# A sample's recurrent steps cut in two, and mixed with the last chunk of a head

## The chip, the cores and the metric

The kernel runs on one core of a Trainium2 chip. The metric is the device time of one execution in microseconds. Its engines are named as in the profile: PE is TensorE's matmuls and PEld its weight loads, DVE is VectorE, ACT is ScalarE, POOL is GpSimd, and SP is SyncE, which issues most of the transfers.

## The reference

The kernel computes one step of a two-layer decoder for a prompt of 2048 positions and eight samples of four tokens each (32 rows). Layer A, in which the change lies, is a gated linear attention with four heads, keys of 128 and values of 512. Per head the prompt runs from a zero state; each sample starts from a stored state of its own.

```python
log_a = log_sigmoid(g_low @ w_gate2 + b_gate) / 16
# per chunk of positions, per head
b   = cumsum(log_a)
rel = where(causal, b[t] - b[s], -inf)
scores[t, s] = sum_d q[t, d] * k[s, d] * exp(rel[t, s, d])
out   = (q * exp(b)) @ state + scores @ v
state = exp(b_last) * state + (k * exp(b_last - b)).T @ v
# per head: RMS norm of out, then
y = (norm(out) * silu(gate)) @ w_out
```

Layer B (windowed attention on shared keys and values) follows; the change does not touch it. Outputs are both groups' activations, the new states and the new caches.

## The kernel before, in words

Products are done in f16 with each f32 operand split in a high and a low part (`split`, lines 194 and 195, or 197 and 198 with a scale: ACT writes the high part, then DVE the low one), in three passes of matmuls. All matmuls are issued through line 101.

Layer A walks over 16 blocks: four heads, and for each the four blocks of 512 positions of the prompt, in the loop over `blocks`. A block projects `q` and `k` (`pj`, copied out at line 430 as `qT`, `kT`), `v` and the gate (`v` is a `split`; the gate's `sg` is a tanh at line 477 and a product at 478), computes the decay's running sum in `logs` (Abs, Exp and Ln on ACT at lines 366 to 368, a sum, a product and a scan on DVE at 370 to 372), the scores by levels, and then four chunks of 128 positions. A block's products are woven (`weave(main, fill)`: the fill's steps spread evenly among the main's) with the next block's levels and with the chunk before.

The last block of a head also makes `SampleA(h)`: the head's projections for the 32 sample rows (`proj_steps`), and a list of steps for their recurrence:

- `diag`: the sample's decay logs (`logs` with 32 columns, tile `E` 128x32, scan into `sbt`), the split of q and k, and the diagonal of the scores `S`;
- `level(0, 2)` and `level(1, 1)`: exponents of decay differences (`k1`, shown as `k`), an Exp on ACT (line 723), products with q and k, the split into `ssm` (194 and 195), three matmuls into `lev`, and a copy into `S`;
- `mid`: the scores' split `Sh`, q with its decay, Exp at line 741, and the factors `ebs`;
- `stack`: keys and values stacked for three passes, transposed, and the first matmul into the readout `o`;
- eight times `seq(b)`: load of the sample's state (`W`, two samples in one transfer; in the last head `bt`, one each), its split into `pst`, three matmuls of it into `o`, one for the update into `kv`, the decay of the state on ACT (line 795), the sum on DVE, and the store;
- `fin`: norm and gate, into `ogTs`.

The first four steps are put behind the last chunk's steps of the head (`prev_tail`) and woven with the `v` and `sg` projections of the next head's first block; the other ten are spread over that block's three remaining chunks. In the last head all of them go into the steps of the output projection.

Two things set the order of the work around the change. Each engine runs its queue in order, so that an instruction which waits holds all behind it on that engine. And the queues themselves come from a scheduler that takes the program's order as priority: an instruction stands where its inputs and buffers are expected, the earlier step first; some steps (the conversion of later weights, through `pst` and `pre`) are put 200 places back in priority. Buffers are few: two PSUM buffers `pj`, one each of `lev` and `kv`, two of `tr` and `o`, two `E`, two `pst`, twelve `W`, three `wraw`, one `S`, one `ssm`, one `sq2`, two `bt`.

Weights come in through `wraw` (issued on SP at line 223), are scaled and split into `W` (197 and 198), and free `wraw` for the next load. A state load of the sample stands behind such loads on SP.

Of the kernel before, what the change touches and what calls it, by code (L numbers as in the profile page):

```python
# [74 lines left out]
def _body(tc, nc, cp, sb, ps, dr, i, o):  # L75
# [6 lines left out]
    def T(tag, shape, dt, bufs=None):  # L82
        return sb.tile(shape, dt, tag=tag, name=nm(tag), **({} if bufs is None else {"bufs": bufs}))

    def PT(tag, shape, dt=F32, bufs=1):
        return ps.tile(shape, dt, tag=tag, name=nm(tag), bufs=bufs)
# [582 lines left out]
    class SampleA:  # L669
# [18 lines left out]
        def steps(self):  # L688
# [6 lines left out]
            def dup3(t, src):  # L695
                split((t[:, 0], t[:, 1]), src.unsqueeze(1).to_broadcast([P, 3, SMP]))
                return t

            def diag():
                if h == 0:  # L700
                    ogTs[0] = T("ogTs", [P, 16, 2, SMP], F16, 1)
                bx["bt"] = T("sbt", [P, SMP], F32, 1)
                logs(gls, h, SMP, rms, bx["bt"])
                qs, ks = self.qkv[:, 0, :], self.qkv[:, 1, :]
                S = bx["S"] = T("S", [96, SMP], F32, 1)
                X0 = dup3(T("ssm", [P, 2, 3, SMP], F16, 1), ks)
                X1 = dup3(T("sq2", [P, 2, 3, SMP], F16, 1), qs)
                pd = PT("lev", [P, 512])
                for n, (a, b) in enumerate(PASSES):
                    mm(pd[:96, :SMP], f(X0, a), X1[:, b, 0, :], start=n == 0, stop=n == 2)  # L710
                dve.tensor_tensor(S, pd[:96, :SMP], id3, ALU.mult)

            def level(li, m):
                bt, S = bx["bt"], bx["S"]
                qs, ks = self.qkv[:, 0, :], self.qkv[:, 1, :]
                vw = lambda t: vw_(t, m)
                btv = vw(bt)
                ref = btv[:, :, 0, m - 1 : m].to_broadcast([P, SMP // 2 // m, m])
                E = T("k1", [P, SMP], F32, 2)
                Ev = vw(E)  # L720
                dve.tensor_tensor(Ev[:, :, 0, :], ref, btv[:, :, 0, :], ALU.subtract)
                dve.tensor_tensor(Ev[:, :, 1, :], btv[:, :, 1, :], ref, ALU.subtract)
                act(E, E, AF.Exp, scale=1.0 / 16)
                dve.tensor_tensor(Ev[:, :, 0, :], Ev[:, :, 0, :], vw(ks)[:, :, 0, :], ALU.mult)
                dve.tensor_tensor(Ev[:, :, 1, :], Ev[:, :, 1, :], vw(qs)[:, :, 1, :], ALU.mult)
                X = dup3(T("ssm", [P, 2, 3, SMP], F16, 1), E)
                pl = PT("lev", [P, 512])
                pv = pl[:96, :16].rearrange("p (B m) -> p B m", m=m)
                for n, (a, b) in enumerate(PASSES):
                    mm(pv, f(X, a), vw(X[:, b, 0, :])[:, :, 1, :], start=n == 0, stop=n == 2)  # L730
                dve.copy_predicated(vw(S)[:, :, 1, :], lvs[:, li, :].rearrange("p (B m) -> p B m", m=m), pv)
# [46 lines left out]
            def seq(b):  # L778
                if h == AH - 1:
                    sr = T("bt", [P, 512], F32, 2)  # L780
                    nc.sync.dma_start(sr, i["state_gla"][0, b, h])
                else:
                    if b % 2 == 0:
                        bx["sr"] = T("W", [P, 2, 512], F32, NW)
                        nc.sync.dma_start(bx["sr"], i["state_gla"][0, b : b + 2, h].rearrange("b p v -> p b v"))
                    sr = bx["sr"][:, b % 2]
                sh = T("pst", [P, 2, 512], F16, 2)
                split((sh[:, 0], sh[:, 1]), sr, SST)
                for n, (a, z) in enumerate(PASSES):
                    mm(bx["po"], bx["qm"][:, a, b : b + 4, :].rearrange("p b t -> p (b t)"), sh[:, z], start=False, stop=b == NS - 1 and n == 2)  # L790
                km = T("skn", [96, P], F16, 2)
                dve.tensor_scalar(km, bx["kst"], bm[:, b : b + 1], None, ALU.mult)
                pkv = PT("kv", [P, 512])
                mm(pkv, km, bx["vst"], start=True, stop=True)
                act(sr, sr, AF.Copy, scale=bx["ebl"][:, b : b + 1])
                dve.scalar_tensor_tensor(sr, pkv, 1.0 / (SQ * SQ), sr, ALU.mult, ALU.add)
                if h == AH - 1:
                    nc.sync.dma_start(o["st_s"][0, b, h], sr)
                elif b % 2:
                    nc.sync.dma_start(o["st_s"][0, b - 1 : b + 1, h].rearrange("b p v -> p b v"), bx["sr"])  # L800

            def fin():
                po = bx["po"][:SMP]
# [10 lines left out]
                dve.tensor_tensor(sg, pt, sg, ALU.mult)  # L814
                split((ogTs[0][:, h * 4 : h * 4 + 4, 0, :], ogTs[0][:, h * 4 : h * 4 + 4, 1, :]), sg)

            return [diag, lambda: level(0, 2), lambda: level(1, 1), mid, stack] + [lambda b=b: seq(b) for b in range(NS)] + [fin]

    def out_w(w, half, gs):
        return Cols(w, half * 512, 512, gs, 4)  # L820
# [121 lines left out]
    for n, (h, j) in enumerate(blocks):  # L942
# [99 lines left out]
        prev_tail = cur.chunk_steps(3) + (nxt.decay_steps() if nxt else [])  # L1042
        if j == NBL - 1:
            sparts = samp.steps()
            prev_tail += sparts[:4]
            del sparts[:4]
            if nxt is None:
                prev_tail += sparts
        cur = nxt
# [794 lines left out]
```

## Time and profile before

| | |
|---|---|
| median of three runs | 2862.65 us (2855.01, 2862.65, 2867.41) |
| profiled execution | 2863.85 us, its span 2862.1 us |
| granted clock of TensorE, mean | 0.983 |
| PE busy | 2735.9 us (96%), 19070 matmuls |
| DVE, ACT, POOL busy | 64%, 50%, 37% |
| transfers | 391.78 MB, 137 GB/s in the mean |
| layer A's heads | up to about 1180 us; a head is some 275 us |

The profile of one execution lists each instruction with its start and its length, by the program's line and tile name. A matmul group's row reads "out<-in, partitions x elements, xcount". Idle time in front of an instruction is shown in brackets with what ended it. Because TensorE is busy for almost the whole span, its own idle places are what to look for; idle time of another engine matters where one of those places waits for it. The sample's steps stand near 330 to 400 us for the first head, 600 to 670 for the second, 880 to 945 for the third, and after 1180 for the last.

### The profile page before, as it was taken

Reading aid. Unit: us, or ns where it says so; the run is one execution under the profiler, and the core shown is the slowest. Engines: PE = TensorE matmul, PEld = TensorE weight load, DVE = VectorE, ACT = ScalarE, POOL = GpSimd, SP = SyncE. Lnnn points to the kernel's source line nnn. Section 1 sums busy time; section 2 is a strip of 40 time slices with the busy share of each in tenths; the row PEclk is TensorE's granted clock in tenths of the full one; section 3 lists DMA queues with packets and bytes.
Section 4 is the critical chain, followed back from the end, with each engine's and each line's share of the span. In section 5 each row is a group of like instructions: output and inputs, shape, how many; then the busy total and the mean of one; then the engine's idle time right before and its main releaser. Section 6 shows DMA issues by size and latency. Waiting matters only on the chain.

```text
span 2862.1 us, 51609 instructions
## 1 busy us (share of the span) xinstructions
PE 2735.9 (96%) x19070; PEld 1392.4 (49%) x19070; DVE 1845.7 (64%) x3815; ACT 1440.3 (50%) x3385; POOL 1063.6 (37%) x1471
## 2 busy tenths in 40 slices
PE   6899999999999999999899999999999999988999
PEld 3445444444454444444344555555555555543444
DVE  5767787677768775336413666677777766767653
ACT  6655665466546654333313555566666666641110
POOL 1242233222322321116405676666566556530000
PEclk9899999999999999999999999999999999999999
DMA  8351334124312533799975555866877788798651
GB/s 209 90 124 36 100 101 150 38 82 136 115 38 85 171 84 96 180 240 282 233 193 135 108 130 120 203 117 129 173 116 130 157 155 165 151 236 172 125 112 57
DMA packets 774230, 391.78 MB, mean 137 GB/s; under 512 B 629200, under 2 KB 698776, under 8 KB 773944
## 3 DMA queue, kind: packets, MB, share of 16 engines
q1 hardware_dynamic: 761016, 352.75, 54.6%
q0 software_dynamic: 10880, 35.66, 3.4%
q8 instruction: 149, 2.44, 0.4%
q14 instruction: 105, 0.86, 0.1%
q10 hardware_dynamic: 2080, 0.07, 0.0%
HBM read 138.90 MB, written 107.54 MB: 86 GB/s over the span
## 4 chain that ended last, share of the span: by engine, by line
PE 56%; DVE 12%; DMA 11%; ACT 10%; issue 6%; POOL 4%; SPq 1%; DVEq 0%; ACTq 0%; POOLq 0%
PE pj L101 33%; PE o L101 11%; PE tr L101 8%; PE kv L101 3%; ACT o L1279 2%; DMA pst<-v 2%; DVE v L198 2%; ACT v L197 2%; DMA pre<-pst 1%; PE lev L101 1%; DMA wraw<-in_a_w_in_dram 1%; DVE o L1274 1%; DVE W L198 1%; POOL ogT L195 1%; DVE lev L1274 1%
## 5 line engine op out<-in xcount | busy, mean ns | idle before, releaser
L101 PE MATMUL pj<-W,uT 128*128 128x512 f16 x5088 | 1208.1, 383 | 6.6 <-ACT qT L430 2.9
L101 PEld LDWEIGHTS <-uT 128*128 128x128 f16 x6976 | 654.7, 99 | 714.1 <-issue 40.4
L101 PE MATMUL tr<-W,uT 128*128 128x512 f16 x1536 | 365.8, 379 | 0.0
L186 POOL TENSOR_SCALAR rs_m<-ss 128x1 f32<-128x1 f32 (+3 forms) x190 | 46.1, 243 | 685.7 <-ACT og L611 234.0
L101 PEld LDWEIGHTS <-X 128*128 128x128 f16 x2744 | 185.8, 98 | 149.3 <-issue 14.7
L1279 ACT ACTIVATE o<-o,mx 128x256 f32<-128x256 f32 (+1 forms) x384 | 168.5, 439 | 168.1 <-DVE mx L1274 163.6
L1274 DVE CUSTOM_DVE_ANT_0 o<-o,madd,nsink 128x256 f32<-128x256 f32 (+1 forms) x384 | 184.0, 479 | 48.3 <-PE o L101 44.0
L101 PE MATMUL pj<-uT,W 128*128 128x512 f16 (+1 forms) x912 | 186.0, 354 | 27.0 <-DMA uT<-ogT 24.3
L198 DVE SCALAR_TENSOR_TENSOR v<-o,v 128x512 f16<-128x512 f32 (+1 forms) x192 | 128.8, 671 | 102.0 <-ACT v L197 82.0
L187 POOL TENSOR_TENSOR rs_r<-rs_m,mhalf 128x1 f32<-128x1 f32 (+2 forms) x186 | 184.8, 994 | 14.4
L101 PEld LDWEIGHTS <-W 128*128 128x128 f16 x2448 | 128.0, 98 | 113.1 <-issue 18.5
L101 PEld LDWEIGHTS <-v 128*128 128x128 f16 x976 | 95.2, 98 | 116.0 <-DMA v<-ogd 1.9
L508 POOL TENSOR_TENSOR E<-bt 128x256 f32<-128x256 f32 x96 | 73.9, 770 | 198.4 <-DVE X L195 124.8
L195 POOL TENSOR_TENSOR ogT<-og,ogT 128x512 f16<-128x512 f32 x68 | 88.0, 1295 | 154.4 <-ACT ogT L194 142.5
L101 PEld LDWEIGHTS <-sth 128*128 128x128 f16 x2080 | 111.4, 99 | 52.3 <-DMA sth<-v 12.2
L101 PEld LDWEIGHTS <-sg 128*128 128x128 f16 x800 | 78.6, 99 | 107.5 <-DMA sg<-ogd 12.3
L101 PE MATMUL o<-gl,X 128*128 128x256 f16 (+1 forms) x768 | 114.9, 273 | 5.5 <-DMA X<-qe 5.5
L197 ACT ACTIVATE v<-o 128x512 f16<-128x512 f32 (+1 forms) x192 | 111.3, 579 | 11.1 <-DMA sth<-v 7.6
L101 PE MATMUL kv<-rmask,sth 128*128 128x64 f16 x1984 | 107.0, 194 | 10.1 <-DMA sth<-v 9.2
L101 PE MATMUL kv<-rmask,pst 128*128 128x64 f16 x992 | 102.4, 194 | 9.3 <-DMA pst<-v 9.3
L1279 ACT ACTIVATE lev<-lev,mx 128x256 f32<-128x256 f32 (+1 forms) x128 | 56.5, 441 | 103.3 <-DVE mx L1274 101.2
L101 PE MATMUL pj<-W,v 128*128 128x512 f16 x448 | 104.2, 379 | 1.1 <-DMA v<-ogd 1.1
(468 smaller groups left out, 5092.5 us busy)
## 6 DMA issues: line engine op xcount, KB each, us to landing
pre<-pst POOLq DMA_DIRECT2D x72, 256.0 KB, 3.4
W<-pre SPq DMA_DIRECT2D x36, 512.0 KB
ogd<-ogT SPq DMA_DIRECT2D x68, 256.0 KB
wraw<-in_a_w_in_dram SPq DMA_DIRECT2D x64, 256.0 KB
wraw<-in_b_w_in_dram SPq DMA_DIRECT2D x64, 256.0 KB
oge<-ogT SPq DMA_DIRECT2D x64, 256.0 KB
wraw<-in_a_w_out_dram SPq DMA_DIRECT2D x32, 256.0 KB
X<-in_x_prompt_dram SPq DMA_DIRECT2D x32, 256.0 KB
```

The costliest lines, as they stand in the source:

```text
L101: return order(nc.tensor.matmul(*a, **k))
L186: pool.tensor_scalar(m[:n, :k], ss, a, b, ALU.mult, ALU.add)
L187: pool.tensor_tensor(r[:n, :k], m[:n, :k], mhalf[:n, :k], ALU.pow)
L195: eng.tensor_tensor(lo, src, hi, ALU.subtract)
L197: act(hi, src, AF.Copy, scale=sc)
L198: dve.scalar_tensor_tensor(lo, src, sc, hi, ALU.mult, ALU.subtract)
L508: pool.tensor_tensor(Ev[:, :, 0, :], ref, btv[:, :, 0, :], ALU.subtract)
L1274: dve.tensor_tensor_reduce(pm[:, z], pm[:, z], madd.rearrange("p a b -> p (a b)")[:, (2 - nk) * P :], -0.125, nsink[:, g * GRP + h : g * G ...
L1279: act(pm[:, z], pm[:, z], AF.Exp, scale=-1.0, bias=nm_[:, h : h + 1], accum_out=bx["sum"][:, h : h + 1])
```

## The change

`diag`, `level` and `seq` are cut in two: the first half makes the operands, the second (`diag_2`, `level_2`, `seq_2`) does the products and what follows from them. A step `turn(b)` makes the operands of sample b + 1 and then does the products of sample b; the operands of sample 0 are made together with `stack`. The list of a head's end has seven steps instead of four, and it is mixed step by step with the last chunk's steps and the next block's decay steps, where it was appended to them. Ten steps remain to be spread over the next block, as before.

```diff
-                pd = PT("lev", [P, 512])
+                bx["X"] = X0, X1
+
+            def diag_2():
+                (X0, X1), S = bx["X"], bx["S"]
+                pd = PT("lev", [P, 512])
                 for n, (a, b) in enumerate(PASSES):
                     mm(pd[:96, :SMP], f(X0, a), X1[:, b, 0, :], start=n == 0, stop=n == 2)
...
-                X = dup3(T("ssm", [P, 2, 3, SMP], F16, 1), E)
+                bx["X"] = dup3(T("ssm", [P, 2, 3, SMP], F16, 1), E)
+
+            def level_2(li, m):
+                X, S = bx["X"], bx["S"]
...
                 split((sh[:, 0], sh[:, 1]), sr, SST)
+                bx["s", b] = sr, sh, bx.get("sr")
+
+            def seq_2(b):
+                sr, sh, both = bx.pop(("s", b))
...
+            def turn(b):
+                if b + 1 < NS:
+                    seq(b + 1)
+                seq_2(b)
+
+            head = [diag, diag_2, lambda: level(0, 2), lambda: level_2(0, 2), lambda: level(1, 1), lambda: level_2(1, 1), mid]
+            return head + [lambda: (seq(0), stack())] + [lambda b=b: turn(b) for b in range(NS)] + [fin]
...
-            prev_tail += sparts[:4]
-            del sparts[:4]
+            prev_tail = mix(prev_tail, sparts[:7])
+            del sparts[:7]
```

Every engine has the same instructions as before, in another order; TensorE's order differs only at the head ends and in the steps after them. Three places follow, in the order in which the queue holds the rows. (In the new file the lines from 711 on are shifted: 366 to 368 and 477 are as before, 723 is 727, 741 is 749, 795 is 807.)

ScalarE, end of head 2, before: the last gate tanh `sg` of the prompt's projections, weight splits, and far later the sample's logs.

```order
L194 ACTIVATE X_6731<-E_6725 128x512
L611 ACTIVATE og_6827,ss_6828<-o_6625 128x512
L477 ACTIVATE sg_6785<-pj_6748 128x512
L197 ACTIVATE W_6880<-wraw_6881,gsa 128x512
L197 ACTIVATE W_6880<-wraw_6885,gsa 128x512
L194 ACTIVATE ogT_6846<-og_6827 128x512
L194 ACTIVATE X_6793<-E_6788 128x512
```

The same place with the change; `E_6923` is the sample's tile for its logs.

```order
L194 ACTIVATE X_6731<-E_6725 128x512
L611 ACTIVATE og_6827,ss_6828<-o_6625 128x512
L366 ACTIVATE E_6923<-tr_6921,bgate 128x32
L367 ACTIVATE E_6923<-E_6923 128x32
L368 ACT_TABLE_LOAD
L368 ACTIVATE E_6923<-E_6923,one_b 128x32
L477 ACT_TABLE_LOAD
L477 ACTIVATE sg_6785<-pj_6748 128x512
L197 ACTIVATE W_6880<-wraw_6881,gsa 128x512
L197 ACTIVATE W_6880<-wraw_6885,gsa 128x512
```

The sample's logs with two table loads have moved up by some 15 places, to stand ahead of `sg` and the weight splits. The two loads are gone from the place in front of `qT`.

VectorE, end of head 2, before: `ssm_7000` is the operand of the first level, `bt_7058` the next block's running sum of decays.

```order
L724 TENSOR_TENSOR k_1194_7011<-k_1194_7011,sqk_6310 128x16
L725 TENSOR_TENSOR k_1194_7011<-k_1194_7011,sqk_6310 128x16
L371 SCALAR_TENSOR_TENSOR E_7065<-E_7065,E_7061 128x512
L195 TENSOR_TENSOR ssm_7000<-k_1190_6994,ssm_7000 128x96
L372 SCALAR_TENSOR_TENSOR bt_7058<-rmask_78,E_7065 128x512
```

With the change, where that operand is `ssm_6968`:

```order
L370 TENSOR_SCALAR E_7065<-tr_7059,bgate 128x512
L371 SCALAR_TENSOR_TENSOR E_7065<-E_7065,E_7061 128x512
L372 SCALAR_TENSOR_TENSOR bt_7058<-rmask_78,E_7065 128x512
L715 TENSOR_TENSOR S_6931<-lev_6945,id_1589 96x32
L195 TENSOR_TENSOR ssm_6968<-k_1182_6962,ssm_6968 128x96
```

The low half of `ssm` now stands behind the scan of line 372 (which these lists print as a SCALAR_TENSOR_TENSOR), where it stood ahead of it.

ScalarE, block 1 of the next head, before (the part after the first head):

```order
L430 ACTIVATE kT_4872<-pj_4847 128x512
L197 ACTIVATE pst_5356<-wraw_5357,gsb 128x512
L197 ACTIVATE X_4933<-E_4931 128x512
L194 ACTIVATE ogT_4923<-og_4911 128x512
L510 ACTIVATE E_4955<-E_4955 128x512
L197 ACTIVATE pst_5366<-wraw_5367,gsb 128x512
L197 ACTIVATE v_4927<-pj_4874 128x512
L194 ACTIVATE X_4961<-E_4955 128x512
```

And with the change:

```order
L430 ACTIVATE kT_4872<-pj_4847 128x512
L197 ACTIVATE pst_5212<-wraw_5213,gskv 128x512
L197 ACTIVATE X_4933<-E_4931 128x512
L510 ACT_TABLE_LOAD
L510 ACTIVATE E_4955<-E_4955 128x512
L197 ACTIVATE pst_5222<-wraw_5223,gsb 128x512
L194 ACTIVATE ogT_4923<-og_4911 128x512
L194 ACTIVATE X_4961<-E_4955 128x512
L197 ACTIVATE v_4927<-pj_4874 128x512
```

The load to the Exp table stood ahead of an earlier `sg` and now stands at the first Exp of line 510; `v_4927` has gone behind `X_4961`, and the weight conversions (`pst`) come some three later.

## What the change was predicted to do

> **What bounds the kernel now.** I read the page's busy line first, then TensorE's waits grouped by what ended them, then the timelines of the places where those waits lie.
>
> ```profile
> PE 2735.9 (96%) x19070; PEld 1392.4 (49%) x19070; DVE 1845.7 (64%) x3815; ACT 1440.3 (50%) x3385; POOL 1063.6 (37%) x1471
> core 0: 2862.1 us, clock 0.983
> PE lev L101 <- ACT ssm L194: 7.4, 4, 2.5
> PE pj L101 <- ACT qT L430: 2.9, 3, 1.6
> PE o L101 <- DVE pst L198: 0.7, 2, 0.3
> PE o L101 <- DVE ke L774: 0.5, 1, 0.5
> ```
>
> The last four rows are total, count and longest (us). TensorE is busy 96% of the span, so its instructions set the end and a change that keeps all 19070 matmuls can win back only its idle time. The four waits for `ssm` are the four `level(0, 2)` products of the sample (one per head); `pst` and `ke` are the waits of the `seq` and `stack` products. These are what the change names: 7.4 + 0.7 + 0.5 = 8.6 us, 0.3% of the span. The `qT` row lies beside them. Here is the end of head 2, TensorE and then ScalarE (start, duration, instruction; in brackets the idle time before it and what ended it):
>
> ```profile
> 625.21 5.56 PE L101 MATMUL pj<-uT,W 128*128 128x512 f16 x25
> 632.33 0.59 PE L101 MATMUL pj<-W,uT 128*128 128x512 f16 x2 [1.56 <-ACT qT L430]
> 634.54 0.25 PE L101 MATMUL lev<-ssm 128*96 128x16 f16 x1 [1.62 <-ACT ssm L194]
> ```
>
> ```profile
> 607.16 0.60 ACT L477 ACTIVATE sg<-pj 128x512 f32<-128x512 f32 x1 [0.24 <-PE pj L101]
> 608.46 1.33 ACT L197 ACTIVATE W<-wraw,gsa 128x512 f16<-128x512 f32 x2 [0.70 <-PE pj L101]
> 617.93 0.63 ACT L197 ACTIVATE pst<-W 128x512 f16<-128x512 f32 x1 [4.02 <-DMA W<-in_state_gla_dram]
> 623.43 0.29 ACT L366 ACTIVATE E<-tr,bgate 128x32 f32<-128x32 f32 x1
> 623.62 0.59 ACT L197 ACTIVATE v<-pj 128x512 f16<-128x512 f32 x1
> 624.10 0.23 ACT L367 ACTIVATE E<-E 128x32 f32<-128x32 f32 x1
> 624.86 1.28 ACT L368 ACT_TABLE_LOAD   x1
> 626.16 0.32 ACT L368 ACTIVATE E<-E,one_b 128x32 f32<-128x32 f32 x1
> 632.30 1.28 ACT L368 ACT_TABLE_LOAD   x1
> ```
>
> So the wait for `ssm` is a wait for ScalarE's queue: after `v` at 623.62 it goes through two table loads in the rows shown (a third, of L723, lies between), and `qT` and `ssm` come late out of it. The other heads look alike:
>
> ```profile
> 358.75 0.21 PE L101 MATMUL lev<-ssm 128*96 128x16 f16 x1 [2.53 <-ACT ssm L194]
> 904.89 0.59 PE L101 MATMUL pj<-W,uT 128*128 128x512 f16 x2 [0.98 <-ACT qT L430]
> 907.10 0.25 PE L101 MATMUL lev<-ssm 128*96 128x16 f16 x1 [1.62 <-ACT ssm L194]
> 1182.07 0.21 PE L101 MATMUL lev<-ssm 128*96 128x16 f16 x1 [1.62 <-ACT ssm L194]
> ```
>
> **What it removes.** With every operand made a step ahead and the two loads in front of `qT` gone, all of this could vanish: `ssm` 2.53 + 1.62 + 1.62 + 1.62 = 7.39, `qT` 1.56 + 0.98 = 2.54, `pst` and `ke` 0.7 + 0.5 = 1.2 (the groups); together **-11.1 us**. The instructions are the same in kind and number on every engine, table loads included (41), so nothing else is removed.
>
> **What it adds.** The order of the ScalarE queue shows the price. The sample's decay logs (L366, L367, load, L368) with the load back to Exp now stand ahead of `sg` at 607.16, instead of around `v` at 623.62. By the rows above these five take 0.29 + 0.23 + 1.28 + 0.32 + 1.28 = 3.4 us, or about 3.1 by their start spacing (neighbouring activations overlap by some 0.1). Queued behind them are `sg`, the weight splits `W<-wraw`, and everything after. In head 2 TensorE's own lateness gives back 0.24 + 0.70, which leaves about 2.5; in head 1 next to nothing (3.1).
>
> The splits free the raw weight buffers, on which SyncE's queue waits, and the sample's state load is issued behind those weight loads; that order is unchanged:
>
> ```profile
> 610.02 0.33 SPq L223 DMA_DIRECT2D wraw<-in_a_w_in_dram  x1
> 611.40 0.42 SPq L785 DMA_DIRECT2D W<-in_state_gla_dram  x1
> 342.80 0.63 ACT L197 ACTIVATE pst<-W 128x512 f16<-128x512 f32 x1 [1.42 <-DMA W<-in_state_gla_dram]
> ```
>
> The state was issued at 611.40 and released ScalarE at 617.93, 6.5 us later. Issued 2.5 us later it lands, at the same flight time, 2.5 us later, and ScalarE's 4.02 us of waiting, which looks like room for the moved logs, is no room: its end moves with them. The `pst` split of the state is still ahead of `ogT`, `qe` and `v`, so the whole queue is late. Two more items now stand before `v`: the stack's 128x384 copy, which I put at 0.5 from the 128x512 copies' 0.6, and two `k` activations of 0.23, while L366's 0.29 is gone. So `v` is late by the state's lateness plus some 0.5: 3.6 us in head 1, 3.0 in heads 2 and 3. What is waiting for `v` is the PSUM buffer that its split frees, and the `pj` block at 625.21 takes it:
>
> ```profile
> 624.37 0.72 DVE L198 SCALAR_TENSOR_TENSOR v<-pj,v 128x512 f16<-128x512 f32 x1
> 349.18 0.69 DVE L198 SCALAR_TENSOR_TENSOR v<-pj,v 128x512 f16<-128x512 f32 x1
> 351.09 2.10 PE L101 MATMUL pj<-uT,W 128*128 128x512 f16 x9
> 897.42 1.28 ACT L368 ACT_TABLE_LOAD   x1
> 898.36 5.56 PE L101 MATMUL pj<-uT,W 128*128 128x512 f16 x25
> ```
>
> VectorE's half of `v` ends at 625.09, 0.1 us before that block; in head 1 at 349.87, 1.2 us before. In head 3 the load at 897.42 follows `v` by the same 1.24 us as in head 2 (623.62 to 624.86), which puts the end of VectorE's half at 897.65, 0.7 before. New waits for `v`: 3.6 - 1.2 = 2.4, 3.0 - 0.1 = 2.9, 3.0 - 0.7 = 2.3, together **+7.6** (from 0, if the state lands in time, to 3 x 3.6 = 10.8).
>
> Later the queue has two loads and the short items fewer (about 3.4 us), so `qT` is in time. But the low half of `ssm` moves on VectorE, from ahead of the block's scan to behind it:
>
> ```profile
> 634.96 0.25 DVE L195 TENSOR_TENSOR ssm<-k,ssm 128x96 f16<-128x96 f32 x1
> 635.13 1.22 DVE L372 TENSOR_TENSOR_SCAN bt<-rmask,E 128x512 f32<-128x512 bf16 x1
> ```
>
> The product now waits for 1.22 of scan more than its operands need. From 0 (cover by the `pj` matmuls ahead) to 1.2 + 0.25 in each of three heads; TensorE arrives there late itself, but nothing else is left to run, so I take 1.2, near the upper end: **+3.6**.
>
> In block 1 of the next head (three times) the load to the Exp table moves from an early `sg` to the first L510, and `v` goes behind an `X` that waits for VectorE. Before, after head 1:
>
> ```profile
> 426.04 1.28 ACT L477 ACT_TABLE_LOAD   x1
> 446.98 0.58 ACT L197 ACTIVATE v<-pj 128x512 f16<-128x512 f32 x1
> 449.27 0.63 ACT L194 ACTIVATE X<-E 128x512 f16<-128x512 f32 x1 [1.72 <-DVE E L512]
> 447.60 0.38 PE L101 MATMUL kv<-v,ke 128*128 128x512 f16 x1 [0.56 <-ACT v L197]
> 450.83 0.58 PE L101 MATMUL kv<-v,ke 128*128 128x512 f16 x1 [2.42 <-DVE v L198]
> ```
>
> At 426 the load is covered by idle time behind it; at 445 it is on the way to `v`. `v` can be late by 1.28 + 1.72 + 0.6 = 3.6, but TensorE already waits 2.42 right behind for VectorE's half, and would pause once instead of twice. Per head from -0.7 (better packing, the 0.56 gone) to 2.0; I take 0.7: **+2**.
>
> **The clock.** These windows (PE, PEld, DVE, ACT, POOL busy, then granted clock) follow pauses:
>
> ```profile
> 450.00:455.00 5.00, 4.17 (x10) 1.43 (x10) 4.43 (x11) 2.48 (x5) 3.36 (x3) 0.50 0.57 184
> 635.00:640.00 5.00, 5.00 (x21) 2.22 (x20) 3.71 (x13) 3.24 (x8) 0.85 (x2) 0.76 0.00 0
> 360.00:365.00 5.00, 5.00 (x27) 2.34 (x26) 3.62 (x13) 3.12 (x8) 0.77 (x2) 1.00 0.00 0
> ```
>
> After head 2's two pauses the clock lost 0.24 x 5 = 1.2 us on top of them; after head 1's single 2.53 nothing (1.00 from 360 on). Two pauses per head remain with the change, though elsewhere, so I keep the dips and add **+1** for head 1 (0 to 1.2).
>
> Sum: -11.1 + 7.6 + 3.6 + 2 + 1 = **+3.1 us** on the profiled execution's 2863.85 (span 2862.1 and 1.75 around it), 2867. The median of three runs, 2862.65, is 1.2 below that execution: **2866 us**, 0.1% slower, which is no change that shows.
>
> On one price the Trainium skill differs. "ScalarE: Activation LUTs", section "What ACT_TABLE_LOAD costs", adds a drain of about 1.38 us to a load of 1.283. Here the load at 624.86 takes 1.28 and the next activation starts at 626.16, 1.30 after it; the trace does not agree. With a switch of 2.66 the logs would delay `sg` by an estimated 2.7 us more, and three heads would add 8 us, 2874.
>
> **Rivals.** (1) *The state is not late.* If its landing is set by the transfers ahead of it and not by the issue (6.5 us for one load is long), the 4.02 of idle swallows the logs and all waits go: -11.1, head 2's dip of 1.2 and as much for head 3, + 2 for block 1: -11.5, on the median 2851. Where only half goes, 2857. For it: the idle is larger than the 3.1 put in. Against: in head 1 it is only 1.42, and the issues follow the splits.
>
> (2) *Slower: the pauses are answered with a half clock.* After the 2.42 at 450.83 the clock was 0.50 for 5 us, 2.5 us lost. If the wait for `v` at each of three head ends does the same, that is 7.5 instead of the 1 added and 2.4 already there, 4.1 more; and where `v` in block 1 takes its full 2.0 per head, 4 more: 2874, and with the waits for `v` at their bound of 10.8 instead of 7.6, 2877. It decides from pauses of some 2.4 us on. Against: 2.53 at 358.75 cost no clock.
>
> (3) *The change does nothing that shows.* Most instructions are only a few places from where they were, and TensorE's order moves the diagonal's products by three matmuls; the waits shift among the same buffers and sum to the same: 2862.65, within 4.
>
> **How the numbers follow.** The forecast has 0.45 (2859 to 2873), (1) 0.25 (2847 to 2858), (2) 0.17 (2871 to 2885), (3) 0.13. Half a per cent, about what a measurement here can tell, is 14.3 us: below 2848.3 or above 2877. Faster by more takes all of (1) and a bit: 0.10. Slower by more is most of the upper half of (2) and the forecast's rim: 0.12. Within: 0.78. The range is 2850 to 2878, which leaves out the ends of (1) and (2).
>
> **What would show it.** Right: the logs and their two loads ahead of `sg`; the state load's issue some 2.5 us later relative to TensorE's work; a `pj` wait of over 2 us for `v` at three head ends; no `lev<-ssm` wait on ScalarE, but one on VectorE of about a microsecond; the last head's 1.62 and the `pst` and `ke` waits gone. Wrong: the state's landing not later, `pj` running through (rival 1); a clock of 0.5 at the head ends (rival 2); or a stage far from the head ends, the out projection above all, moving by more than 5 us, of which this working has nothing.

## The result, and the profile after

The changed kernel takes 2883.1 us (median of six runs, 2881.9 to 2889.9), the kernel before 2862.3 us beside it (six runs). The ratio is 1.0077, 95% interval 1.0061 to 1.0092: slower by 0.8%, 20.9 us, where 2866 and no visible change were forecast. The profiled execution has a span of 2881.4 us, 19.3 more than before, at a granted clock of 0.986 (0.983 before). TensorE works as long as it did, so the loss in sum is idle time:

```profile
PE 2735.7 (95%) x19070; PEld 1390.7 (48%) x19070; DVE 1850.2 (64%) x3815; ACT 1438.6 (50%) x3385; POOL 1064.5 (37%) x1471
```

TensorE's waits after the change, grouped as before (total us, count, longest):

```profile
PE kv L101 <- ACT v L197: 9.1, 6, 2.1
PE pj L101 <- DVE v L198: 8.4, 5, 2.8
PE lev L101 <- DVE S L531: 7.8, 11, 1.7
PE pj L101 <- DMA v<-ogd: 6.3, 3, 2.9
PE lev L101 <- ACT X L197: 5.6, 3, 3.8
PE o L101 <- ACT pst L197: 5.5, 4, 2.0
```

The rows for `ssm` on ScalarE (7.4) and for `ke` (0.5) are gone, that for `qT` is down from 2.9 to 0.6. New at the top are waits for `v`, for the block's own scores `S` (3.9 before), for `pst` split on ScalarE (there was none), and for the transposed reads of `ogd` (1.1 before).

Where they lie is seen by cutting the span into stages. The waits printed in the timeline, added by place in both profiled executions:

| place | before | after |
|---|---|---|
| head ends 1 to 3 with block 0 (325-425, 600-700, 875-975 us) | 9.5 | 8.5 |
| block 1 behind them (440-492, 700-765, 980-1050) | 9.4 | 20.9 |
| block 2 behind that | 0.8 | 0 |
| last head's sample and first half of the output projection (1130-1300) | 1.6 | 4.9 |
| rest of the output projection (1300-1480) | 13.3 | 16.9 |

That is 16.6 us of the 19.3. The head ends, round which the change is built, came out even. Block 1, which it does not touch, lost 11.5 us, and the last head with the output projection 6.9.

What these stages cost in time, waits and clock together, can be read from work that is the same in both kernels. Each head's projections of the sample rows (`pj<-uTs,W`) are one such place, the last row of TensorE another:

| TensorE's row | starts before | starts after | later by | since the row above |
|---|---|---|---|---|
| head 1, `pj<-uTs,W` | 283.30 | 282.26 | -1.0 | |
| head 2 | 557.59 | 558.72 | 1.1 | 2.2 |
| head 3 | 831.34 | 840.70 | 9.4 | 8.2 |
| head 4 | 1105.05 | 1114.66 | 9.6 | 0.3 |
| layer B, its first `pj<-uTs,W` | 1580.89 | 1600.71 | 19.8 | 10.2 |
| last row, `pj<-uT,sg` | 2857.69 | 2877.09 | 19.4 | -0.4 |

So nearly all of it lies in two places: some 8 us between the projections of heads 2 and 3, and 10 from those of the last head to layer B, with the output projection between. Layer B gives none. The three blocks 1 wait about alike (7.0, 7.5 and 6.4 us, against 3.0, 2.9 and 3.5 before), but the granted clock falls in other places: after head 2 now in four stretches of 5 us (0.85, 0.81, 0.76 and 0.90 from 725, 730, 760 and 765 on, where it was 1.00 before), while the falls that the kernel before has after head 1 (0.50 from 450 on) and after head 3 (0.92 and 0.74 from 995 and 1000 on) are gone.

The same from the busy times. First the three stretches of block 1 summed (440 to 490, 700 to 765, 980 to 1045 us), then the stretch 1180 to 1480, each for the kernel before:

```profile
sum 180.00, PE 170.36 PEld 78.91 DVE 146.90 ACT 113.70 POOL 65.28; mean PE 56.79 PEld 26.30 DVE 48.97 ACT 37.90 POOL 21.76
1180.00:1480.00 300.00, 285.12 (x1542) 132.33 (x1539) 125.78 (x193) 95.19 (x185) 96.07 (x134) 0.98 0.93 226
```

and for the changed one:

```profile
sum 180.00, PE 159.06 PEld 73.03 DVE 148.66 ACT 117.77 POOL 69.76; mean PE 53.02 PEld 24.34 DVE 49.55 ACT 39.26 POOL 23.25
1180.00:1480.00 300.00, 278.21 (x1494) 128.37 (x1492) 125.70 (x173) 92.82 (x178) 96.00 (x136) 0.97 0.91 221
```

Of the same 180 us of block 1 TensorE was busy 170.4 and then 159.1, and of the 300 us of the output projection 285.1 and then 278.2.

**The head end** went the way that the prediction worked out. ScalarE after the change, end of head 2, then TensorE at the three places where it waits for `v`:

```profile
608.14 0.28 ACT L366 ACTIVATE E<-tr,bgate 128x32 f32<-128x32 f32 x1
608.70 1.28 ACT L368 ACT_TABLE_LOAD   x1
610.33 1.28 ACT L477 ACT_TABLE_LOAD   x1
611.62 0.60 ACT L477 ACTIVATE sg<-pj 128x512 f32<-128x512 f32 x1
622.41 0.63 ACT L197 ACTIVATE pst<-W 128x512 f16<-128x512 f32 x1 [4.05 <-DMA W<-in_state_gla_dram]
```

```profile
352.75 1.20 PE L101 MATMUL pj<-uT,W 128*128 128x512 f16 x3 [2.46 <-DVE v L198]
629.61 1.01 PE L101 MATMUL pj<-uT,W 128*128 128x512 f16 x2 [2.83 <-DVE v L198]
909.53 0.59 PE L101 MATMUL pj<-uT,W 128*128 128x512 f16 x2 [1.62 <-DVE v L198]
```

`sg` starts at 611.62 instead of 607.16 (TensorE itself is about 0.6 us late by then), the state is back at 622.41 instead of 617.93, after the same 4 us of waiting for it, and `v` costs 2.46, 2.83 and 1.62 us where 2.4, 2.9 and 2.3 were forecast. That head 2 came out so close is partly luck: ScalarE's half of `v` is later by 4.6 us (628.26 after 623.62), not 3.0, and TensorE comes to the place that needs it some 1.4 us later than before (626.78 after about 625.4, by the spacing in its row at 625.21), not at the same time.

**Block 1.** After head 2, all of TensorE's waits before the change:

```profile
724.12 0.38 PE L101 MATMUL kv<-v,ke 128*128 128x512 f16 x1 [1.45 <-ACT v L197]
726.08 0.59 PE L101 MATMUL kv<-v,ke 128*128 128x512 f16 x2 [0.50 <-DVE v L198]
734.80 1.24 PE L101 MATMUL pj<-W,uT 128*128 128x512 f16 x5 [0.23 <-DVE sg L478]
739.05 0.38 PE L101 MATMUL kv<-v,ke 128*128 128x512 f16 x1 [0.72 <-ACT v L197]
```

With the change, ScalarE and then four of TensorE's seven waits:

```profile
722.77 1.28 ACT L510 ACT_TABLE_LOAD   x1
724.60 0.71 ACT L197 ACTIVATE pst<-wraw,gsb 128x512 f16<-128x512 f32 x1
727.07 0.58 ACT L197 ACTIVATE v<-pj 128x512 f16<-128x512 f32 x1
```

```profile
722.81 0.18 PE L101 MATMUL lev<-one_h,X 128*128 128x1 f16 x1 [1.19 <-ACT X L197]
727.70 0.38 PE L101 MATMUL kv<-v,ke 128*128 128x512 f16 x1 [2.10 <-ACT v L197]
752.07 0.51 PE L101 MATMUL lev<-X 128*128 128x64 f16 x12 [1.67 <-DVE S L531]
761.81 0.38 PE L101 MATMUL kv<-v,ke 128*128 128x512 f16 x1 [1.06 <-DVE v L198]
```

The first `v` is late by an amount that the forecast allows (2.10 after 1.45 before). But the waits go on through the block, 30 and 40 us behind the table load, on VectorE as well as on ScalarE, and for tiles that the prediction had not looked at.

**The output projection.** The last head's samples now make TensorE wait three times for their split states, 4.9 us together. Of the transposed reads, the wait for `sg` is a little shorter (8.19 after 9.36), those for `v` are longer (0.84, 2.56 and 2.87 after 0.17 and 0.97), and behind the last of them the clock falls to 0.50, so that the same 46 matmuls take 13.02 us instead of 10.10. The kernel before, and then the changed one:

```profile
1384.07 1.04 PE L101 MATMUL pj<-W,sg 128*128 128x512 f16 x2 [9.36 <-DMA sg<-ogd]
1412.22 10.10 PE L101 MATMUL pj<-W,v 128*128 128x512 f16 x46 [0.97 <-DMA v<-ogd]
```

```profile
1239.32 0.38 PE L101 MATMUL o<-pst,qe 128*128 128x512 f16 x1 [1.29 <-ACT pst L197]
1245.18 0.38 PE L101 MATMUL o<-pst,qe 128*128 128x512 f16 x1 [2.03 <-ACT pst L197]
1252.79 0.38 PE L101 MATMUL o<-pst,qe 128*128 128x512 f16 x1 [1.59 <-ACT pst L197]
1397.61 1.03 PE L101 MATMUL pj<-W,sg 128*128 128x512 f16 x2 [8.19 <-DMA sg<-ogd]
1429.12 13.02 PE L101 MATMUL pj<-W,v 128*128 128x512 f16 x46 [2.87 <-DMA v<-ogd]
1430.00:1435.00 5.00, 5.00 (x13) 1.76 (x12) 0.69 (x1) 0.72 (x2) 0.00 (x0) 0.50 1.12 280
```

### The profile page after: what moved, and what is told of

It reads as the page before. It is cut to its first block, busy times and chain, and to the rows that moved or that the text cites. A ratio compares the mean times of both kernels' runs of the same rounds, so it can differ in the third digit from the quotient of the medians.

```text
span 2881.4 us, 51601 instructions
## 1 busy us (share of the span) xinstructions
PE 2735.7 (95%) x19070; PEld 1390.7 (48%) x19070; DVE 1850.2 (64%) x3815; ACT 1438.6 (50%) x3385; POOL 1064.5 (37%) x1471
## 4 chain that ended last, share of the span: by engine, by line
PE 57%; DVE 12%; DMA 11%; ACT 9%; issue 5%; POOL 4%; SPq 2%; ACTq 0%; DVEq 0%; POOLq 0%
PE pj L101 34%; PE o L101 11%; PE tr L101 8%; PE kv L101 3%; ACT o L1297 2%; DVE v L198 2%; DMA wraw<-in_a_w_in_dram 1%; ACT v L197 1%; DMA pst<-v 1%; PE lev L101 1%; DVE W L198 1%; DVE o L1292 1%; DMA pre<-pst 1%; POOL ogT L195 1%; DVE X L195 1%
## 5 line engine op out<-in xcount | busy, mean ns | idle before, releaser
L187 POOL TENSOR_TENSOR rs_r<-rs_m,mhalf 128x1 f32<-128x1 f32 (+2 forms) x186 | 187.9, 1011 | 14.4
L101 PEld LDWEIGHTS <-sg 128*128 128x128 f16 x800 | 78.6, 99 | 105.4 <-DMA sg<-ogd 10.2
```

The costliest lines, as they stand in the source:

```text
L101: return order(nc.tensor.matmul(*a, **k))
L187: pool.tensor_tensor(r[:n, :k], m[:n, :k], mhalf[:n, :k], ALU.pow)
```

## The experiments

Each verdict is a ratio to the kernel before on the same chip, with its 95% interval. Waits of block 1 are the sum over the same three stretches as in the table above; the idle time of the output projection is 300 us less TensorE's busy time between 1180 and 1480 us (14.9 before, 21.8 with the change). Both are read from one profiled execution of each kernel, and single executions of a kernel lie 5 to 18 us apart here, so a microsecond or two of waits between two kernels says little.

### Which part costs: the lookahead, the mixing, the last head

Four kernels undo parts of the change. The lookahead alone (the head's four steps whole and appended):

```diff
-            head = [diag, diag_2, lambda: level(0, 2), lambda: level_2(0, 2), lambda: level(1, 1), lambda: level_2(1, 1), mid]
+            head = [lambda: (diag(), diag_2()), lambda: (level(0, 2), level_2(0, 2)), lambda: (level(1, 1), level_2(1, 1)), mid]
...
-            prev_tail = mix(prev_tail, sparts[:7])
-            del sparts[:7]
+            prev_tail += sparts[:4]
+            del sparts[:4]
```

> Only the lookahead of the samples (operands of sample b+1 ahead of the products of sample b, operands of sample 0 with the stack); the four steps of the head's end are whole again and appended. The changed kernel lost 20.9 us, some 10 of it in block 1 after heads 1 to 3 and some 10 in the output projection. Theory S (the lookahead is at fault: it holds the two pst buffers and the two bt buffers a step longer, so weight conversions and the last head's state loads come late): about 2880, with block 1's waits near 20 us in sum. Theory H (the head's end is at fault: the early logs, the moved Exp load, the later start of the last head): 2861, block 1's waits near 10 us.

The head's end alone, mixed:

```diff
-            return head + [lambda: (seq(0), stack())] + [lambda b=b: turn(b) for b in range(NS)] + [fin]
+            return head + [stack] + [lambda b=b: (seq(b), seq_2(b)) for b in range(NS)] + [fin]
```

> Only the head's end: diag and levels cut in two and mixed with the last chunk; the samples one by one as before. Theory S: 2862 to 2866 (new waits for v of 7 us at the head ends against 7 of ssm and 2.5 of qT that go). Theory H: 2880 to 2883.

The same with its seven steps appended:

```diff
-            prev_tail = mix(prev_tail, sparts[:7])
+            prev_tail += sparts[:7]
```

> As head_only, but the seven steps are appended to the last chunk's steps, not mixed with them. Theory S: 2862 or a little less. Theory H, if it is the mixing that moves the logs ahead of the gate's tanh and starts the last head later: 2858 to 2863 here, against 2880 in head_only. If cutting diag and level in two is itself what costs: as head_only.

The whole change without the lookahead in the last head:

```diff
+            if h == AH - 1:
+                return head + [stack] + [lambda b=b: (seq(b), seq_2(b)) for b in range(NS)] + [fin]
             return head + [lambda: (seq(0), stack())] + [lambda b=b: turn(b) for b in range(NS)] + [fin]
```

> The whole change, but the last head's samples one by one as before (its state loads go through the two bt buffers). Theory S: the output projection's loss of some 10 us goes, 2873. Theory H: 2883, the last head's products still wait for their pst (4.9 us in three waits).

| kernel | us | ratio (interval) | waits in block 1 | idle, output projection |
|---|---|---|---|---|
| the change | 2883.1 | 1.0077 (1.0061 to 1.0092) | 20.9 | 21.8 |
| lookahead alone | 2870.3 | 1.0046 (1.0027 to 1.0065) | 20.9 | 14.2 |
| head's end alone, mixed | 2871.4 | 1.0051 (1.0033 to 1.0068) | 14.2 | 19.2 |
| head's end alone, appended | 2860.8 | 1.0004 (0.9989 to 1.0019) | 9.0 | 13.7 |
| change, last head's samples as before | 2874.9 | 1.0061 (1.0039 to 1.0083) | 18.8 | 16.5 |

Neither theory stands alone: the lookahead costs 0.46% and the mixing 0.51%. Cutting `diag` and `level` in two costs nothing that shows, as long as the pieces are appended. The lookahead in the last head is worth 0.16%, 4.6 us, by the ratios (the medians are 8.2 apart, but the kernel before beside them differs too, 2862.3 and 2859.2; the intervals overlap), and it goes with most of the output projection's idle time, 21.8 to 16.5.

### What makes block 1 wait

Theory P said that the lookahead holds the two `pst` buffers, so that the weight conversions, which use them too, start late. In heads 1 to 3 the samples' split states were put in `W` buffers instead, in the change and, as the measure for it, in the kernel before:

```diff
-                sh = T("pst", [P, 2, 512], F16, 2)
+                if h < AH - 1:
+                    if b % 2 == 0:
+                        bx["sh2"] = T("W", [P, 2, 2, 512], F16, NW)
+                    sh = bx["sh2"][:, b % 2]
+                else:
+                    sh = T("pst", [P, 2, 512], F16, 2)
```

> The whole change, but in heads 1 to 3 the split states of the samples go into W buffers (two samples in one), so the two pst buffers are left to the weight conversions and to stack and fin. Theory P (the lookahead holds pst, the conversions start late, at 418 instead of 412 us after head 1, and end in block 1's last chunk beside its v): block 1's waits of TensorE fall from 20.9 us to some 10, 2873. Theory O (the order on ScalarE does it: the Exp load at L510, v behind X): they stay near 20, 2883.

> The kernel before with the same placement of the samples' split states in W buffers, as the measure for sh_in_w. Both theories: 2855 to 2862, block 1's waits at 10 us or somewhat less.

The change: 2868.3 us, 1.0044 (1.0028 to 1.0061), 15.6 us of waits in block 1, where P had 10 and O 20. The kernel before with the same placement: 2868.6 us, 1.0028 (1.0015 to 1.0042), 17.3 us of waits. So the change's loss against its measure nearly goes, but not as P said: the measure itself became slower, and its block 1 waits even longer than the change's.

The conversions were then shared out otherwise over a head's blocks (`PR`, the number of them per chunk in blocks 0 to 3):

```diff
-PR = (1, 4, 2, 0)
+PR = (1, 2, 4, 0)
```

> The whole change with the weight conversions shared out otherwise: two instead of four per chunk in block 1, four instead of two in block 2 of each head. If the conversions beside block 1's chunks are what makes v late (P, or any other reason for their lateness): block 1's waits fall from 20.9 to 10 to 13 us, 2873 to 2876, unless block 2 takes the same waits over. Theory O: block 1's waits stay near 20 us, 2883.

> The kernel before with conversions shared out as in change_pr (two per chunk in block 1, four in block 2). Block 1's waits, with 16, 18 and 8 conversions there by the order, 9.4 us before, fall to 5 to 8; the measure for change_pr (2877.7). If fewer conversions beside block 1 help the kernel before too: 2850 to 2856; if the waits move on to block 2: 2858 to 2863.

2877.7 us for the change, 1.0065 (1.0045 to 1.0085), waits of 11.9 in block 1 and 3.9 in block 2; 2875.1 for the kernel before with it, 1.0046 (1.0030 to 1.0061), waits of 15.9. In the three stretches ScalarE starts 11, 17 and 5 conversions, where the kernel before starts 10, 15 and 7; it waits more in all three, also in the last, where there are fewer (5.5, 5.5 and 4.9 us against 3.0, 2.9 and 3.5).

With none in block 0, where the samples' steps run, in the kernel with the lookahead alone and in the kernel before (`PR = (0, 4, 3, 0)`):

> The lookahead alone, with no weight conversions in block 0 of heads 2 to 4 (where the samples' steps run) and three instead of two per chunk in block 2; block 1 keeps its four per chunk. If a conversion that takes the second pst buffer between two samples is what makes the last sample late and with it block 1's conversions: block 1's waits as in base_pr0, within 2 us, and the two kernels within 3 us. If the order on ScalarE does it: block 1's waits near 20 us here, 10 in base_pr0, and 8 us or more between them.

> The kernel before with the same sharing of conversions, the measure for seq_pr0: 2855 to 2865, block 1's waits 8 to 12 us.

2867.7 us, 1.0039 (1.0025 to 1.0052), waits of 20.1; and 2866.6 us, 1.0040 (1.0026 to 1.0054), waits of 17.9, not 8 to 12. The lookahead, which alone cost 0.46%, costs nothing here, because the kernel before has lost as much.

With more of them early, in the kernel before (`PR = (2, 3, 2, 0)`):

> The kernel before with two conversions per chunk in block 0, three in block 1, two in block 2 (by the order 4, 4 and 2 stand in block 0 and 15, 17 and 13 in block 1, against 3, 2, 1 and 16, 18, 14). If early conversions are what keeps block 1 free: waits there of 5 to 8 us, 2852 to 2858. If conversions among the samples' steps delay these: 2860 to 2868.

2873.4 us, 1.0045 (1.0030 to 1.0061), waits of 13.7. In the profile two, four and four conversions start before the last sample's split state is made after heads 1 to 3, against none, two and two before, block 1's stretches hold 9, 15 and 7, hardly other than before, and its waits are still longer. Lateness of the conversions by itself is not what sets them; theory P is dropped.

Whether the conversions are needed for the waits at all was tried by leaving none in layer A's blocks behind the first head; all run in the output projection (`PR = (0, 0, 0, 0)`):

> The whole change with no weight conversions in layer A's blocks after the first head's end; all of them run in the output projection. If block 1's waits (20.9 us in the change) are conversions standing ahead of v, X and the level copies in the queues of ScalarE and VectorE: below 6 us in sum here, and the difference to base_none before the output projection is only the head ends (within 3 us). If it is the order of block 1's own work (the Exp load at L510, v behind X): 12 us or more, and 8 us or more above base_none.

> The kernel before with no weight conversions in layer A's blocks, the measure for change_none. Block 1's waits below 6 us; the output projection, which is full of transfers, grows by 10 us or more.

The change takes 2931.3 us, 1.0260 (1.0243 to 1.0277), the kernel before 2928.1, 1.0254 (1.0239 to 1.0269). The three stretches of block 1, the change first:

```profile
sum 180.00, PE 180.00 PEld 86.04 DVE 114.23 ACT 86.78 POOL 36.59; mean PE 60.00 PEld 28.68 DVE 38.08 ACT 28.93 POOL 12.20
```

```profile
sum 180.00, PE 180.00 PEld 86.00 DVE 115.36 ACT 88.66 POOL 38.84; mean PE 60.00 PEld 28.67 DVE 38.45 ACT 29.55 POOL 12.95
```

TensorE is busy for all 180 us in both. In both the table load stands at the first L510 (435.48 and 435.56 after head 1) and `v` behind `X`: this order, on which the prediction had put its 2 us, costs nothing without conversions beside it. Nor does the place of the load decide with conversions. In the lookahead with `PR = (0, 4, 3, 0)` it stands at the early `sg` after all three heads, as in the kernel before, and block 1 waits 20.1 us; in the change with `PR = (1, 2, 4, 0)` it stands at L510, and block 1 waits 11.9. After head 1, in this order:

```profile
427.89 1.28 ACT L477 ACT_TABLE_LOAD   x1
447.78 1.28 ACT L510 ACT_TABLE_LOAD   x1
```

So theory O, that the order of block 1's own work does it, is dropped too, as far as the load goes. VectorE has 114 us of work in the stretches without conversions and 149 with them, ScalarE 87 and 118, and the transfers that belong to the conversions are gone as well (DMA share of the three stretches 0.09, 0.08 and 0.19, with them 0.55, 0.59 and 0.62); which of these makes TensorE wait was not separated. Put off to the output projection the conversions cost far more than here: both kernels are 72 to 75 us slower than the kernel before. Most of that falls at the projection's end and right behind it, with single waits up to this one of the kernel before without conversions in layer A:

```profile
1595.46 6.66 PE L101 MATMUL pj<-W,uT 128*128 128x512 f16 x24 [33.30 <-DVE qT L1179]
```

### The head end: the two table loads

The change with the logarithm of the 32 sample columns left out, so that its two table loads go and the order of the rest stays:

> The whole change, but the sample's decay logs copy where they took the Ln (left out: the logarithm of the 32 sample columns), so the two table loads ahead of the gate's tanh are gone and the rest of the order stands. If the loads delay the weight splits, through them the state load and through it v, as forecast: the three waits of TensorE for v at the head ends, 2.46, 2.83 and 1.62 us, fall below 0.7 each, and the state is back some 2.5 us earlier; block 1's waits stay near 20 us; 2870 to 2877. If the wait for v has another cause: it stays, 2880.

```diff
+        if n == SMP:
+            act(t[:, :n], t[:, :n], AF.Copy)
+        else:
             act(t[:, :n], t[:, :n], AF.Ln, bias=one_b[:, 0:1])
```

2872.1 us, 1.0049 (1.0033 to 1.0065). ScalarE at the end of head 2, and TensorE at the `v` waits (the third is gone):

```profile
604.84 0.28 ACT L366 ACTIVATE E<-tr,bgate 128x32 f32<-128x32 f32 x1
605.55 0.58 ACT L480 ACTIVATE sg<-pj 128x512 f32<-128x512 f32 x1
616.46 0.63 ACT L197 ACTIVATE pst<-W 128x512 f16<-128x512 f32 x1 [4.12 <-DMA W<-in_state_gla_dram]
622.36 0.58 ACT L197 ACTIVATE v<-pj 128x512 f16<-128x512 f32 x1
349.31 0.81 PE L101 MATMUL pj<-uT,W 128*128 128x512 f16 x3 [0.25 <-DVE v L198]
623.72 0.59 PE L101 MATMUL pj<-uT,W 128*128 128x512 f16 x2 [1.05 <-DVE v L198]
```

With the two loads gone, `sg` starts 0.71 us after the logs' first instruction (3.48 with them: 608.14 to 611.62), and the three waits for `v` shrink from 6.9 us to 1.3 (1.05 in head 2, where less than 0.7 was expected). So the chain of the forecast, loads, weight splits, state load, `v`, is shown. The waits of block 1 stay at 19.5; the waits at the head ends are not their cause. The profiled execution is the fastest of this kernel's five (2863.4 us, median 2872.1), and in it TensorE idles 14.4 us in the output projection, no more than in the kernel before, though the last head runs all the steps of the change but the Ln.

### The last head

The change in heads 1 to 3, with the last head's steps all as before; and the head's end alone, mixed in heads 1 to 3 and appended in the last:

```diff
-            prev_tail = mix(prev_tail, sparts[:7])
+            prev_tail = mix(prev_tail, sparts[:7]) if nxt else prev_tail + sparts[:7]
```

> The change in heads 1 to 3, the last head's steps as before (appended, samples one by one). With the samples alone as before in the last head it was 8.2 us less than the change. If the mixing, too, costs there (its stack came 12 us later): 2870 to 2872, the out projection's loss gone altogether. If not: 2875.

> Only the head's end, mixed in heads 1 to 3 and appended in the last. head_only was 10.6 us slower than head_append; by the times of single stages 6 of it lay behind the last head's start. If so: 2865. If the last head's mixing costs nothing: 2871.

The first: 2873.3 us, 1.0049 (1.0035 to 1.0062), idle time of the output projection 16.1 of 300 us. The second: 2871.9 us, 1.0058 (1.0043 to 1.0073), idle 14.6, where the same with the last head mixed was 1.0051 and idle 19.2. Restoring the last head takes back some 8 of the change's 20.9 us by the ratios in the first comparison, and most of the idle time in both; but in the second the whole time does not follow (block 1's waits rose from 14.2 to 16.8 in its profile though the program of those heads is the same). And the three waits for the samples' split states are not the lookahead's alone: with the last head all as before they are 1.44, 0.34 and 0.82 us. The last head's share is so between 0 and 10 us, no better known.

## Why the prediction was wrong, point by point

**What bounds the kernel** was right: the instructions are the same, TensorE's busy time is the same to 0.2 us, and in sum the loss is TensorE's idle time.

**What is removed**, 11.1 us: the waits for `ssm` on ScalarE, for `ke` and, at the head ends, for `qT` are gone (the 0.6 left for `qT` is one wait in the first head's start). The 0.7 for `pst` is not: TensorE now waits 5.5 us for split states on ScalarE, 4.9 of them in the last head.

**The wait for `v`**, +7.6, measured 2.46 + 2.83 + 1.62 = 6.9, by the way that was worked out; removing the two loads showed the way. That ScalarE's 4 us of waiting for the state were no room held: the wait was 4.05 after the change and 4.12 without the loads, its end moved. The state moved by 4.5 us on the clock of the trace, 3.9 beside TensorE's work, not 2.5; that the waits came out near their price nonetheless is partly luck, as shown above.

**The low half of `ssm`**, +3.6, did not show. After heads 1 and 2 TensorE comes to the product, late from its wait for `v`, when the low half is done (360.15 after 359.30, 636.51 after 635.89). After head 3 it waits 0.51 us there, by the row for `S` (line 715), which stands behind the scan.

**The clock**, +1 in head 1: the granted clock was 0.80 and 0.86 in the two 5 us stretches after the 2.46, 1.7 us lost; it had been bounded at 1.2. But the fall after head 3, which the prediction kept (0.70 and 0.95 in the stretches from 905 and 910 on before), is gone (1.00 and 1.00), so that the clock of the three head ends together came out even.

**Block 1**, +2 with bounds of -0.7 to 2.0 per head, is the step that failed. It measured 11.5 us of waits, 3.8 per head, nearly twice its upper bound. The prediction priced one table load and one `v` that goes behind one `X`, in a few rows of ScalarE after the first head. For the rest of the block it has no term, although the order of the queue, on record with it, had the weight conversions come some three later; it put that at nothing without a reason. In time the heads lose 10.7 us from the first one's projections to the last's, where the terms of the sum up to there give 4.7. What the runs show in its place: without conversions in the block the waits are 0 in both kernels, with them they go on through the whole block, on VectorE as on ScalarE, and they come also in kernels that leave the samples' steps alone and only deal the conversions or buffers anew.

**The output projection**, for which the sum had only -1.6, is the other failed term: 6.9 us of idle time more. With the clock behind it that is 10.2 us of time from the last head's projections to layer B, and under the other tables 4 to 10. The prediction says of a move of more than 5 us there that its working has nothing of it, and named it as a sign that it was wrong. Its cause stays open.

**The rivals.** (1) did not happen; (2), slower, had the right sign and block 1 as one of its two places, and the measured time lies in the range given to it; but that is luck. Its 2874 to 2877 come from a halved clock at the head ends, which came out even, and from `v` at its bound of 2.0 us per head in block 1. (3) did not happen either.

**What the pairs say.** With each other way of sharing out the conversions that was tried, the difference between a kernel and its measure is small: with `PR = (1, 2, 4, 0)` 1.0065 / 1.0046, 0.19%; the states in `W` 1.0044 / 1.0028, 0.16%; no conversions 1.0260 / 1.0254, 0.06%; the lookahead alone, none in block 0, 1.0039 / 1.0040, nothing. That is -0.3 to 5.4 us, each uncertain by some 6 to 7, and the forecast's +3.1 is among them. Only against the kernel before as it stands is it 20.9. And that kernel loses 0.28 to 0.46% by each of the four edits that share out its conversions or buffers anew and leave the samples' steps alone (2.5% by the fifth, no conversions in layer A).

The small differences are sums of two larger ones. By the starts of `pj<-uTs,W`, as in the second table above, the profiled executions of each pair differ so:

| a kernel over its measure | from head 1's to head 4's, us | from head 4's to layer B's, us |
|---|---|---|
| the change over the kernel before | +10.7 | +10.2 |
| both with `PR = (1, 2, 4, 0)` | -4.1 | +10.4 |
| both with the states in `W` | -4.7 | +3.9 |
| both without conversions in layer A | -6.8 | +6.9 |
| the lookahead alone, both with `PR = (0, 4, 3, 0)` | +1.4 | -3.4 |

In heads 1 to 4 the whole change is faster than its measure in three of four pairs, and slower only beside the kernel before as it stands. From the last head on it is slower in all four. A reading that fits these, and is argued rather than shown, is that the numbers of the table fit one order of the queues; a change of order, this one or another, loses the fit, and so the loss in the heads has little to do with what was changed. The loss in the output projection comes with the change under every table tried, though not in the run without the Ln (+1.0). These are single executions, in which 4 us alone say little; what counts is that the pairs agree. The one part of the change that costs nothing, the cut steps appended, is the one whose block 1 waits as before (9.0 against 9.4).

**What stays open** is which conversion ahead of which instruction makes the difference. Lateness and number of the conversions and the place of the table load do not order the kernels by their waits, and no run here moved single conversions with all else held. Nor is the last head's part settled better than 0 to 10 us, nor why the output projection loses. No kernel tried was faster than the one before.

## What to carry to other kernels

Where a scheduler orders full queues, a moved step re-deals what comes after it, in stages that the edit does not name: compare the order of every engine to the end of the disturbed stretch and price the filler work in it (here conversions on ScalarE and VectorE), not only the instruction on the path. A table of numbers that shares out filler work may suit one order alone; judge an edit also against the old kernel with the table changed, which helps to tell what the edit itself costs from what a lost fit costs. And idle time of an engine that waits for a load is no room for work that the load's issue waits for.

## What the hardware showed that was not expected

VectorE's instructions of one form and size can take more than twice as long as they mostly do. In block 1 after head 2 of the changed kernel, VectorE first, then GpSimd:

```profile
720.42 1.67 DVE L491 TENSOR_TENSOR E<-qT,kT 128x512 f32<-128x512 f32 x1
726.19 1.64 DVE L198 SCALAR_TENSOR_TENSOR pst<-wraw,gsb,pst 128x512 f16<-128x512 f32 x1
```

```profile
720.19 0.69 POOL L248 DMA_DIRECT2D pre<-pst  x1 [1.75 <-DVE pst L198]
720.78 0.75 POOL L508 TENSOR_TENSOR E<-bt 128x256 f32<-128x256 f32 x1
725.90 1.38 POOL L195 TENSOR_TENSOR ogT<-og,ogT 128x512 f16<-128x512 f32 x1 [0.25 <-ACT ogT L194]
```

The product of line 491 takes 1.67 us here and 0.69 before the change (at 718.17), a conversion's low half 1.64 where its median is 0.75. Both run while GpSimd is at work on tiles of its own. That the one causes the other was not tried. Such long conversions are no news of the change: of 74 low halves 3 take over a microsecond before it and 4 after it. The product of line 491 takes over 0.9 us once in 16 before it and four times after it; none of this was in a term of the sum.

The granted clock fell after single waits of 2.46 us (0.80 in the 5 us from 350 on) and 2.83 us (0.71 from 630 on), and before the change not after one of 2.53 at 358.75 (1.00). The length of the wait alone does not decide. The Trainium skill, "TensorE: Matmul & The Clock Gate", Part 1, has the clock halved after at least one idle window of about 3.4 us; here single waits shorter than that were followed by a lower clock, so on the length the traces do not agree.
